# Keeping the low parts of the input weights in device memory between token blocks

## The chip, the cores and the metric

The kernel runs on one core of one Trainium2 chip. The metric is the device time of one execution in microseconds (us). The core has five engines with queues of their own: TensorE (PE in the profile, its weight loads PEld), VectorE (DVE), ScalarE (ACT), GpSimd (POOL) and SyncE (SP). SP issues every DMA of this kernel, in order, and 16 DMA engines carry them out.

## The reference

One inference step of a one-layer streaming encoder, for 2048 new frames with 16 meta tokens ahead of them, and for 32 frames of a running stream. All of it is float32.

```python
q, k, v, z_a, b_g, c_g, u, z_c = split_proj(rmsnorm(hp, norm_g[l]), w_in[l])   # 1024 -> 8 x 512
a = softmax(q1 k1/8 + bias) - lam * softmax(q2 k2/8 + bias)      # chunk-causal, 4 heads
o = rmsnorm(a @ v, subln_g) * 0.2 * silu(z_a)
y_c = silu(z_c) * b_g * conv3(c_g * u)                           # causal, width 3
hp = hp + concat(o, y_c) @ w_out                                 # then a final RMSNorm
```

The outputs are the two streams' results, the new keys and values, and the last two rows of the convolution's input.

## The kernel before, in words

**Split products.** TensorE multiplies in a reduced form of float32 (`F32R`). To keep the accuracy, each operand is split in two: a high part, the value cast to `F32R`, and a low part, the value minus the high part. A product is then three matmuls: high x high, high weight x low input, low weight x high input (lines 216 to 218).

**Blocks and columns.** The tokens are handled in four blocks (`p` = 0 to 3): the first holds the meta tokens, 512 frames and the 32 sample frames, the others 512 frames each. In every block all of `w_in` is used, in 32 columns of 128 output channels. One column is 1024 x 128 values, 512 KB, and 24 matmuls of 512 moving columns (in the first block 48 shorter ones). The order is written out in the main loop: for each head `h`, `unit_a` projects the columns q, k, v and z of that head (columns `h`, 4+`h`, 8+`h`, 12+`h`), `attend` does the attention of the block against all earlier keys, and `unit_c` projects four columns of the convolution branch. After the last block the output product (`out_first`, `out_rest`) follows.

**Weights.** `w_load(col, p)` brings in one column (line 190) into one of two `wraw` buffers and splits it in two halves of four 128 x 128 weight tiles each: ACT casts the high part `wh` (line 196), and then `wl = wr - wh` is made by POOL, or by DVE for the columns `CQ` and `CK` (0 and 4) in the first block and `CQ` and `CZ` (0 and 12) in the later ones (line 197). `wh` and `wl` have four buffers each, so two columns: the halves of column n go where those of column n-2 were, once PE has read them. The same is done anew in each of the four blocks.

**Attention.** For each tile of 128 frames and each chunk of keys, PE makes scores in one of three PSUM banks (lines 438, 439), DVE takes the row minimum (lines 385, 388), ACT the exponential out of the bank (line 389), which is what frees the bank. DVE makes the chunk's coefficients (lines 362 to 369), POOL and DVE combine the two softmaxes (lines 392, 393), PE transposes the result (line 454), ACT and DVE split it (lines 457, 458), and PE multiplies by the values (lines 461 to 463). Old keys and values are read back from device memory in each block (`ksd`, `vd`).

**What sets the order.** The kernel is written in Tile. The program order gives priorities, and a scheduler with a cost model of its own lays out a queue for each engine ahead of time (`schedule_with_timeline_sim=True`, line 798); it puts in the semaphores. Projections of the next columns and attention of the current head are so mixed on PE. On the chip each engine, SP too, goes through its queue strictly in that order.

In the trace, PE's first projection matmul of the second block is at about 258 us, of the third at 503, of the fourth at 788, and the output product starts to take over at 1073.

Of the kernel before, what the change touches and what calls it, by code (L numbers as in the profile page):

```python
# [11 lines left out]
F32 = mybir.dt.float32  # L12
F32R = mybir.dt.float32r
AF = mybir.ActivationFunctionType
ALU = mybir.AluOpType
AX = mybir.AxisListType

P = 128
D = 1024
KT = D // P  # L20
# [16 lines left out]
CQ, CK, CV, CZ, CB, CC, CU, CG = range(0, 32, 4)  # L37
# [10 lines left out]
def hybrid_step(ctx: ExitStack, tc: tile.TileContext, x, xT, ckT, cv, scT, rel_bias, norm_g, w_in,  # L48
# [10 lines left out]
    op = pool("op", 3)  # L59
# [3 lines left out]
    dram = pool("dram", 1, space=bass.MemoryType.DRAM)  # L63
# [5 lines left out]
    V, S, G, T = nc.vector, nc.scalar, nc.gpsimd, nc.tensor  # L69
    S.preload_act_table_set("natural_log_exp_and_others")  # L70
    f32 = lambda a: a.bitcast(F32) if a.dtype == F32R else a
    dma = lambda out, in_: nc.sync.dma_start(f32(out), f32(in_))
# [111 lines left out]


    pre = {}

    def w_load(col, p):
        wr = wp.tile([P, KT, P], F32, tag="wraw", name="wr")
        dma(wr, w_in[col])  # L190
        w2 = []
        for i in range(2):
            wh = wp.tile([P, KT // 2, P], F32R, tag="wh", name="wh", bufs=4)
            wl = wp.tile([P, KT // 2, P], F32R, tag="wl", name="wl", bufs=4)
            wi = wr[:, KT // 2 * i:KT // 2 * (i + 1)]
            S.copy(wh, wi)  # L196
            (V if (col in (CQ, CK) if p == 0 else col in (CQ, CZ)) else G).tensor_tensor(wl, wi, f32(wh), op=ALU.subtract)  # L197
            w2.append((wh, wl))
        return w2

    def proj(col, p, evac):
        w2 = pre.pop((col, p), None) or w_load(col, p)
        if p > 0:
            blks = [(0, QT)]
        elif col < CK or CZ <= col < CC or col >= CG:
            blks = [(NM, 288), (288, 560)]
        else:
            blks = [(0, 280), (280, 560)]
        for b0, b1 in blks:
            if p == 0 and col == CV:  # L210
                ps = ps_s.tile([P, 512], F32, tag="s", name="pj")[:, :b1 - b0]
            else:
                ps = ps_j.tile([P, 512], F32, tag="pj", name="pj")[:, :b1 - b0]
            for k in range(KT):
                wh, wl = w2[k // 4]
                for i, (a, b) in enumerate(((wh, xh), (wh, xl), (wl, xh))):
                    T.matmul(ps, lhsT=a[:, k % 4], rhs=b[k][:, b0:b1],  # L217
                             start=(k == 0 and i == 0), stop=(k == KT - 1 and i == 2))
            evac(ps, b0, b1)
# [508 lines left out]
    after = (((0,), (1,), (2, 3), ()), ((0,), (1,), (2,), (3,)))  # L728
    bias_rows()
    pre[CQ, 0] = w_load(CQ, 0)  # L730
    x_load(0)
    load_small()
# [73 lines left out]
```

## Time and profile before

| | |
|---|---|
| median of 3 runs | 1325.01 us (1324.07 to 1325.41) |
| the profiled execution | 1324.97 us |
| its span, first to last instruction | 1323.2 us |
| granted TensorE clock, mean over the span | 0.99 |
| DMA, mean over the span | 150 GB/s, 198.72 MB |
| device memory read, written | 145.62 MB, 43.26 MB |

The profile comes from one execution. Its busy times are unions of instructions on an engine. A matmul's end is modelled and matmuls overlap, so a busy PE is not a PE at its peak; idle time and the distance between starts say more. A row of a timeline has the start and the length in us, the engine, the line, the operation, the tiles written and read, and in brackets the idle time of the engine before it with what ended it.

### The profile page before, as it was taken

What the parts mean: (1) busy time and instruction counts of PE and PEld (TensorE: products, weight loads), DVE (VectorE), ACT (ScalarE), POOL (GpSimd) and SP (SyncE); (2) the same over time, 40 slices, a digit from 0 to 9 for tenths busy, and PEclk for the clock granted to TensorE, in tenths of its full rate; (3) what the DMA queues carried; (4) which work ended last, traced back from release to release, by engine and by line L of the source; (5) the groups of instructions that cost most, each with busy time, mean ns of one, the idle gap of its engine ahead of it and who ended that gap; (6) DMA issues with size and microseconds to landing.
All of it is one profiled execution on the core that took longest, in us unless ns stands there. A gap on an engine that the chain in (4) does not pass through costs nothing.

```text
span 1323.2 us, 21113 instructions
## 1 busy us (share of the span) xinstructions
PE 1279.3 (97%) x7058; PEld 1102.2 (83%) x7058; DVE 1011.5 (76%) x2086; ACT 738.0 (56%) x1854; POOL 731.3 (55%) x659
## 2 busy tenths in 40 slices
PE   8999999999999998999999999999999999999997
PEld 6999899988788886888888788888888887888775
DVE  8766567668797857788878868888798898856754
ACT  6645453664665547566565466565656665654322
POOL 4665655656566664466556656466666575642200
PEclk9999999999999999899999999999999999999999
DMA  9744434674335356534253463344334534557752
GB/s 285 219 141 108 138 99 113 205 243 145 121 105 174 106 159 192 169 127 151 96 168 102 135 194 100 124 131 124 105 104 153 161 110 128 159 183 231 231 176 90
DMA packets 108046, 198.72 MB, mean 150 GB/s; under 512 B 17409, under 2 KB 45601, under 8 KB 107937
## 3 DMA queue, kind: packets, MB, share of 16 engines
q1 hardware_dynamic: 107936, 197.37, 48.4%
q8 instruction: 55, 0.90, 0.3%
q14 instruction: 55, 0.44, 0.1%
HBM read 145.62 MB, written 43.26 MB: 143 GB/s over the span
## 4 chain that ended last, share of the span: by engine, by line
PE 30%; DVE 12%; ACT 3%; issue 2%; POOL 2%; DMA 1%; DVEq 0%; POOLq 0%; ACTq 0%
PE po L686 10%; PE pj L217 10%; DVE p L393 4%; PE pt L454 2%; PE s L438 2%; DVE nm L388 2%; PE s L439 2%; ACT p L389 1%; PE po L462 1%; PE po L463 1%; PE po L461 1%; DVE al L458 1%; POOL wl L197 1%; PE po L678 1%; DMA out<-y 0%
## 5 line engine op out<-in xcount | busy, mean ns | idle before, releaser
L217 PE MATMUL pj<-xh,wh 128*128 128x512 f32 (+2 forms) x1280 | 457.0, 358 | 3.8 <-DVE g L344 1.0
L217 PE MATMUL pj<-xl,wh 128*128 128x512 f32 (+2 forms) x1280 | 455.2, 356 | 1.7 <-DVE xl L145 1.7
L197 POOL TENSOR_TENSOR wl<-wr,wh 128x512 fp32r<-128x512 f32 x240 | 327.7, 1370 | 232.5 <-ACT wh L196 220.6
L217 PE MATMUL pj<-xh,wl 128*128 128x512 f32 (+2 forms) x1280 | 453.5, 355 | 0.0
L389 ACT ACTIVATE p<-s,nm 128x384 f32<-128x384 f32 (+5 forms) x352 | 208.6, 595 | 164.5 <-DVE nm L388 126.0
L217 PEld LDWEIGHTS pj<-xh,wh 128*128 128x128 f32 x1280 | 243.3, 190 | 35.4 <-ACT bvec L596 1.7
L217 PEld LDWEIGHTS pj<-xl,wh 128*128 128x128 f32 x1280 | 242.9, 190 | 30.9 <-DVE xl L145 3.2
L217 PEld LDWEIGHTS pj<-xh,wl 128*128 128x128 f32 x1280 | 242.8, 190 | 30.0 <-issue 1.1
L196 ACT CAST wh<-wr 128x512 fp32r<-128x512 f32 x256 | 157.1, 617 | 99.6 <-PE pj L217 61.4
L393 DVE SCALAR_TENSOR_TENSOR p<-p,cf,p 128x384 f32<-128x384 f32 (+5 forms) x176 | 176.6, 1025 | 21.9 <-POOL p L392 21.2
L392 POOL TENSOR_SCALAR p<-p,cf 128x384 f32<-128x384 f32 (+5 forms) x176 | 122.1, 709 | 60.6 <-DVE cf L369 42.1
L438 PE MATMUL s<-ks,q 128*128 128x384 f32 (+5 forms) x352 | 130.1, 371 | 12.0 <-ACT p L389 11.8
L388 DVE TENSOR_REDUCE nm<-s 128x1 f32<-128x384 f32 (+3 forms) x224 | 121.8, 557 | 2.8 <-PE s L439 2.6
L439 PE MATMUL s<-ks,q 128*128 128x384 f32 (+5 forms) x352 | 123.7, 352 | 0.0
L458 DVE TENSOR_TENSOR al<-pt,ah 128x512 fp32r<-128x512 f32 x144 | 97.0, 681 | 34.6 <-ACT ah L457 34.5
L666 POOL TENSOR_TENSOR cll<-ct,chh 128x512 fp32r<-128x512 f32 x40 | 55.9, 1404 | 108.6 <-ACT chh L664 108.6
L457 ACT CAST ah<-pt 128x512 fp32r<-128x512 f32 x144 | 80.8, 586 | 39.1 <-PE pt L454 36.7
L454 PE MATMUL pt<-ident,p 128*128 128x128 f32 x544 | 88.4, 274 | 1.6 <-DVE p L393 1.4
L438 PEld LDWEIGHTS s<-ks,q 128*128 128x128 f32 x352 | 66.7, 189 | 25.8 <-ACT p L389 18.7
L462 PE MATMUL po<-al,vh 128*128 128x256 f32 x288 | 83.5, 290 | 2.1 <-DVE al L458 2.0
L461 PE MATMUL po<-ah,vh 128*128 128x256 f32 x288 | 81.3, 282 | 0.0
L463 PE MATMUL po<-ah,vl 128*128 128x256 f32 x288 | 81.2, 282 | 0.0
(238 smaller groups left out, 2214.4 us busy)
## 6 DMA issues: line engine op xcount, KB each, us to landing
wr<-in_w_in SPq DMA_DIRECT2D x128, 512.0 KB, 3.7
ct<-cat SPq DMA_DIRECT2D x28, 512.0 KB, 4.6
q<-q SPq DMA_DIRECT2D x64, 128.0 KB, 2.8
out<-y SPq DMA_DIRECT2D x32, 256.0 KB, 3.7
ks<-ksd SPq DMA_DIRECT2D x8, 776.0 KB, 5.2
xr<-in_x SPq DMA_DIRECT2D x24, 256.0 KB, 5.3
out<-g SPq DMA_DIRECT2D x24, 256.0 KB, 2.9
xt<-in_xT SPq DMA_DIRECT2D x24, 256.0 KB, 4.7
```

What stands on the lines that cost most here:

```text
L196: S.copy(wh, wi)
L197: (V if (col in (CQ, CK) if p == 0 else col in (CQ, CZ)) else G).tensor_tensor(wl, wi, f32(wh), op=ALU.subtract)
L217: T.matmul(ps, lhsT=a[:, k % 4], rhs=b[k][:, b0:b1], start=(k == 0 and i == 0), stop=(k == KT - 1 and i == 2))
L388: V.tensor_reduce(nm[:, c, j:j + 1], s, op=ALU.min, axis=AX.X)
L389: S.activation(pr[j][c], s, AF.Exp, bias=nm[:, c, j:j + 1], scale=-1.0, accum_out=l[:, c, j:j + 1])
L392: G.tensor_scalar(a0, a0, cf[:, 0, j:j + 1], 1.0, op0=ALU.mult, op1=ALU.mult)
L393: V.scalar_tensor_tensor(a0, a1, cf[:, 1, j:j + 1], a0, op0=ALU.mult, op1=ALU.add)
L438: T.matmul(ps, lhsT=qd[c][0][:, qs], rhs=ks[c][:, col:col + w], start=True, stop=False)
L439: T.matmul(ps, lhsT=qd[c][1][:, qs], rhs=ks[c][:, col:col + w], start=False, stop=True)
L454: T.transpose(pt[:, i, P * qi:P * (qi + 1)], cols(aa[qi], NM + P * (2 * j + i), P), ident)
L458: V.tensor_tensor(al, pt, f32(ah), op=ALU.subtract)
L686: T.matmul(ps, lhsT=a[k][:, :rows], rhs=b[k], start=(k == 0 and i == 0), stop=(k == KT - 1 and i == 2))
```

## The change

32 tiles of 512 KB are set up in device memory, one for each column. In the second block (`p` = 1) each half of a low part is stored there after it is made. In the third and fourth block (`p` > 1) the low part is no longer computed: each half is loaded from there into the same `wl` buffer by a DMA. The first block is as before, and so are the load of the weights and the cast of the high part in all blocks. The `dma` helper issues on SP.

```diff
     pre = {}
+    wld = [dram.tile([2, P, KT // 2, P], F32, name=f"wld{c}", tag=f"wld{c}") for c in range(32)]
 
     def w_load(col, p):
         wr = wp.tile([P, KT, P], F32, tag="wraw", name="wr")
...
             wl = wp.tile([P, KT // 2, P], F32R, tag="wl", name="wl", bufs=4)
             wi = wr[:, KT // 2 * i:KT // 2 * (i + 1)]
             S.copy(wh, wi)
-            (V if (col in (CQ, CK) if p == 0 else col in (CQ, CZ)) else G).tensor_tensor(wl, wi, f32(wh), op=ALU.subtract)
+            if p > 1:
+                dma(wl, wld[col][i])
+            else:
+                (V if (col in (CQ, CK) if p == 0 else col in (CQ, CZ)) else G).tensor_tensor(wl, wi, f32(wh),
+                                                                                           op=ALU.subtract)
+            if p == 1:
+                dma(wld[col][i], wl)
             w2.append((wh, wl))
         return w2
```

## The prediction

> **What bounds the kernel now.** I read the page first, then the busy time by stage, then what TensorE (PE) waited for, and then the timeline around its longest wait.
>
> ```profile
> span 1323.2 us, 21113 instructions
> PE 1279.3 (97%) x7058; PEld 1102.2 (83%) x7058; DVE 1011.5 (76%) x2086; ACT 738.0 (56%) x1854; POOL 731.3 (55%) x659
> ```
>
> The execution took 1324.97 us: the span and 1.77 us around it. The median of the runs is 1325.01, so a sum made against this execution carries over. PE is the bound. POOL, which loses work here, is idle 45% of the time, so its time cannot be counted as gain. The windows view gives the busy time of each engine, the granted clock, and the share of the DMA engines with their rate, for the second block, the start of the third, the rest of the third, and the fourth:
>
> ```profile
> 258.00:503.00 245.00, 240.54 (x1202) 200.92 (x1203) 191.03 (x401) 143.57 (x358) 152.87 (x130) 0.99 0.50 154
> 503.00:545.00 42.00, 35.49 (x150) 28.54 (x150) 31.58 (x76) 25.86 (x73) 19.16 (x17) 0.88 0.66 216
> 545.00:788.00 243.00, 238.40 (x1262) 203.49 (x1261) 197.92 (x380) 142.90 (x349) 145.47 (x127) 1.00 0.43 136
> 788.00:1073.00 285.00, 282.56 (x1497) 242.15 (x1496) 245.73 (x464) 178.26 (x441) 177.61 (x156) 1.00 0.41 123
> ```
>
> One row stands out: from 503 to 545 us PE is idle for 6.5 of 42 us and its clock is 0.88. Elsewhere in the two blocks that read back, it idles 4.6 and 2.4 us. That is all there is to win: about 13.5 us of idle time and what the clock loses. What these waits end on (total, times, longest), first for the third block, then for the fourth:
>
> ```profile
> PE s L438 <- ACT p L389: 6.6, 5, 3.3
> PE ptv L308 <- DVE g L297: 1.7, 1, 1.7
> PE po L462 <- DVE al L458: 1.3, 1, 1.3
> PE pj L217 <- DVE g L344: 1.0, 1, 1.0
> PE pt L454 <- DVE p L393: 0.4, 1, 0.4
> ```
>
> ```profile
> PE ptv L308 <- DVE g L297: 1.3, 1, 1.3
> PE s L438 <- ACT p L389: 0.5, 1, 0.5
> PE pj L217 <- DVE xl L145: 0.5, 1, 0.5
> ```
>
> No row names wl: the low parts were never late. Every row ends on VectorE (DVE) or on ScalarE (ACT) behind it: the softmax chain (row minimum on DVE, exp on ACT, then a score bank is free) and the copies out of PSUM. So the change can pay only through DVE's lateness.
>
> **What is removed.** The subtraction at L197, by count and by block (second, third, fourth; DVE's part, then POOL's):
>
> ```profile
> L197 POOL TENSOR_TENSOR wl<-wr,wh 128x512 fp32r<-128x512 f32 x240 | 327.7, 1370 | 232.5 <-ACT wh L196 220.6 <-PE pj L217 3.6 <-PE s L439 2.1
> ```
>
> ```profile
> 258.00:503.00 245.00, 4.11 (x4) 82.97 (x61) 0.99 0.50 154
> 503.00:788.00 285.00, 3.83 (x4) 82.24 (x60) 0.98 0.46 148
> 788.00:1073.00 285.00, 2.37 (x2) 81.89 (x60) 1.00 0.41 123
> ```
>
> Two blocks have 2 x 64 = 128 subtractions, 120 on POOL and 8 on DVE (columns 0 and 12). POOL loses 120 x 1.37 = 164 us, half of its work there; DVE loses 8 x 0.95, about 7 us. POOL's part also holds DVE up. The timeline shows it:
>
> ```profile
> 517.27 1.30 POOL L197 TENSOR_TENSOR wl<-wr,wh 128x512 fp32r<-128x512 f32 x1 [1.68 <-ACT wh L196]
> 517.48 1.11 DVE L368 TENSOR_TENSOR r<-r,lam 128x2 f32<-128x2 f32 x1
> 520.58 1.78 DVE L197 TENSOR_TENSOR wl<-wr,wh 128x512 fp32r<-128x512 f32 x1
> 525.01 0.68 DVE L197 TENSOR_TENSOR wl<-wr,wh 128x512 fp32r<-128x512 f32 x1
> 526.95 0.57 DVE L388 TENSOR_REDUCE nm<-s 128x1 f32<-128x400 f32 x1
> 527.55 0.59 ACT L389 ACTIVATE p<-s,nm 128x400 f32<-128x400 f32 x1 [1.71 <-DVE nm L388]
> 528.28 0.59 PE L438 MATMUL s<-ks,q 128*128 128x272 f32 x1 [3.28 <-ACT p L389]
> 529.21 0.16 DVE L368 TENSOR_TENSOR r<-r,lam 128x2 f32<-128x2 f32 x1
> 530.91 0.60 PE L438 MATMUL s<-ks,q 128*128 128x272 f32 x1 [1.80 <-ACT p L389]
> 534.10 0.63 PE L217 MATMUL pj<-xh,wl 128*128 128x512 f32 x1
> 534.53 0.63 PE L217 MATMUL pj<-xh,wh 128*128 128x512 f32 x1
> ```
>
> The same two-element product takes 1.11 us beside a POOL subtraction and 0.16 without one. And the longest wait of the run has two of DVE's own subtractions (1.78 and 0.68) ahead of the row minimum at 526.95, whose exp at 527.55 frees the bank for which PE waits 3.28 us, till 528.28. A second wait of 1.80 follows, and then the clock:
>
> ```profile
> 526.60:536.80 10.20, 6.71 (x19) 5.34 (x20) 9.23 (x29) 4.97 (x15) 4.99 (x7) 0.50 1.01 335
> 150.00:154.50 4.50, 3.56 (x17) 3.26 (x18) 1.90 (x4) 1.84 (x5) 3.16 (x5) 0.63 0.61 175
> ```
>
> For 10.2 us PE has half its clock; matmuls start 0.43 us apart (534.10, 534.53). From 530.91 to 536.8 it works without a gap, 5.9 us that would be 2.9 at full clock: 3.0 us lost. The stretch costs 3.28 + 1.80 + 3.0 = 8.1 us.
>
> *Gain there.* Without the two subtractions DVE's queue is 1.78 + 0.68 = 2.46 us shorter ahead of the minimum; without POOL's at 517.27 the product at 517.48 gives back 1.11 - 0.16, nearly 1.0. That is 3.4 us off the 5.08 us of waits. What is late next is POOL's other work (lines 252 and 278), which also blocks DVE, so the waits do not vanish. Half of the clock's 3.0 should go with them, since a shorter wait may still cost clock: at 150 us a stretch with 0.9 us of idle PE inside it (a wait begun before it) shows 0.63. Total 3.4 + 1.5, say 5 us; bounds 0 (the order is redrawn and another chain is late here) and 8.1.
>
> [...]
>
> *Gain elsewhere.* The other waits are 11.0 - 5.1 = 5.9 us in the third block and 2.3 in the fourth, 8.2 together. They hang on DVE, and POOL's work, whose readers block it, is halved. But the planner lays out a new order for every engine, and new waits come with it; I take a quarter, 2 us (bounds: 8 gained, 4 lost, the size of what the rest of the third block idles now).
>
> **What is added.** In the second block 64 stores of 256 KB, in the third and fourth 128 loads of 256 KB, all on SP. Nearest rows: loads of that size (the whole run's bz, the third block's xr), a store of that size, and one store's issue on SP:
>
> ```profile
> bz<-bz SPq DMA_DIRECT2D x16, 256.0 KB, 3.8
> xr<-in_x SPq DMA_DIRECT2D x6, 256.0 KB, 5.7
> vd<-vl SPq DMA_DIRECT2D x12, 256.0 KB, 4.2
> 528.25 0.43 SPq L72 DMA_DIRECT2D ksd<-ks  x1
> ```
>
> *Stores.* 64 x 0.43 = 28 us of SP's time in 245. Each waits for the POOL subtraction of its half; the next weight load, which SP issues about then, waits for the same subtractions already, so little queued behind is held longer: the q copies, old keys and outputs. The low part's buffer now stays taken until the store has landed, 0.43 + 4.2 after the subtraction, while PE reads it later still (below). Cost 0.5 us (bounds -1 and +4).
>
> *Loads.* A load can start when PE has done with the buffer's last user two columns before, and must land before the third matmul of its half. PE's end of one such use and its first use of the refilled buffer, the closest pair that I found in the third block:
>
> ```profile
> 738.23 0.39 PE L217 MATMUL pj<-xh,wl 128*128 128x512 f32 x1
> 748.23 0.39 PE L217 MATMUL pj<-xh,wl 128*128 128x512 f32 x1
> ```
>
> From 738.62 to 748.23 are 9.6 us. Issue and landing take 0.43 + 3.8 to 0.43 + 5.7, so 3.5 to 5.4 us are spare: cost 0, hidden by the column between. If that cover is gone, each late load is a wait of PE. What eats it is SP, which issues in order (third and fourth block):
>
> ```profile
> SPq L72 <- POOL wl L197: 236.9, 49, 11.6
> SPq L72 <- POOL o L422: 33.0, 7, 10.9
> ```
>
> The first row's waits change their cause: the weight load waits for the cast alone, and the low-part loads for PE. The second shows what a load may be queued behind: 4.7 us on average, 10.9 at most.
>
> **Sum.** 1324.97 - 5 - 2 + 0.5 = 1318.5 us.
>
> **Rivals.**
>
> *The waits only move.* PE's wait for a score bank or a PSUM copy is part of a queue order that is drawn up anew; a DVE that is earlier in one place is idle there and late at another (it is busy 246 of 285 us in the fourth block, where PE still idles just 2.4). For it: wl appears in no wait of PE. Against: the longest wait has the subtractions in its chain. Gain and loss cancel: 1324.5.
>
> *Low parts late, slower.* Place: SP in the third and fourth block, a wl load queued behind a store that waits for POOL or DVE. With 3.5 us spare an average wait of 4.7 makes it 1.2 late, the longest 7.4. From about 9 us in all (the 6.5 us gained and 2.65 more) it decides. Two loads 5 us late, each with a half-clock window (half of 3.4, 1.7 us, the length of such a window taken as a third of the 10.2) cost 13.4: 1318.5 + 13.4 = 1332. Against: most columns have more than 9.6 us, since attention matmuls lie between.
>
> *Transfers bound.* The third block would go from 148 by 16.8 MB / 285 us = 59 to 207 GB/s, well under the 335 reached; but the window from 526.6 is full already (1.01). Two columns' 1 MB there are 3.1 us more at that rate; if PE waits for them and the gain there is lost too, 1324.97 + 3.1 + 0.5, about 1329. Against: prefetches for the fourth block fill that window, and PE's next weights are already in.
>
> [...]
>
> **Chances.** Forecast 0.50; waits only move 0.22; low parts late 0.17; transfers bound 0.06; and 0.05 that nearly all of the 13.5 us and the clock's 3.0 go, about 1309. A measurement of this kernel can tell 0.2%, 2.65 us, from no change: faster 0.55, same 0.22, slower 0.23. The forecast's own range is 1313 to 1322, from its bounds; the range that holds 8 in 10 reaches through the second and fourth case and into the third: 1311 to 1330.
>
> **What would show it.** L197 leaves POOL after about 503 us (POOL near 570 us in all, L197 on POOL x120, on DVE x8); DVE's time falls by more than its own 7 us, with L368 and L393 shorter; PE's 3.28 us wait shrinks and the half clock at the third block's start is shorter or gone; no wait of PE on a DMA of wl; 33.6 MB more read and 16.8 MB more written. Wrong if PE's idle time in the last two blocks stays near 13.5 us though DVE is freed, or if PE rows end on "DMA wl", or if the second block grows by more than 4 us.

## The result and the profile after

The median went from 1325.21 us (1324.07 to 1325.97, 4 runs) to 1307.88 us (1307.37 to 1309.48, 4 runs): 17.3 us less, ratio 0.987 with a 95% interval of 0.9855 to 0.9886. The direction was forecast, the size was not: the time lies below the forecast's range. Of all the runs in this document one was slow, 1555 us at 0.75 of the clock (the kernel in which only the fourth block reads), and the ratios leave it out. The profiled execution took 1309.48 us, 1.8 of it around the span. The page of the kernel after, its span and busy times, and the memory traffic:

```profile
span 1307.7 us, 21292 instructions
PE 1275.0 (98%) x7058; PEld 1103.9 (84%) x7058; DVE 935.7 (72%) x2078; ACT 741.6 (57%) x1854; POOL 562.1 (43%) x539
wl<-wld SPq DMA_DIRECT2D x128, 256.0 KB, 2.8
wld<-wl SPq DMA_DIRECT2D x64, 256.0 KB, 2.5
HBM read 179.17 MB, written 60.04 MB: 183 GB/s over the span
```

POOL lost 169 us of work, and DVE became 76 us shorter, though only eight operations of its own are gone. The span fell by 15.5 us: PE's idle time (span less busy) from 43.9 to 32.7, and its busy time by 4.3, with the same 7058 matmuls: they stand closer together, part of it because less of the time has half clock. By block, cut where the second, third and fourth block's columns and then the output product begin, first the kernel before (its first cut is another than in the prediction), then after:

```profile
258.00:505.50 247.50, 242.02 (x1208) 201.97 (x1209) 193.53 (x406) 144.14 (x358) 154.59 (x131) 0.99 0.51 155
505.50:787.60 282.10, 272.01 (x1403) 230.67 (x1402) 226.60 (x451) 167.79 (x419) 162.50 (x143) 0.98 0.46 147
787.60:1073.30 285.70, 283.26 (x1499) 242.76 (x1498) 246.43 (x464) 178.66 (x442) 178.31 (x156) 1.00 0.41 123
1073.30:1323.20 249.90, 235.12 (x1137) 192.32 (x1135) 169.91 (x350) 113.94 (x301) 84.65 (x71) 0.98 0.53 168
```

```profile
258.00:505.70 247.70, 242.43 (x1210) 201.97 (x1210) 190.54 (x405) 144.42 (x358) 149.83 (x129) 0.99 0.69 225
505.70:776.40 270.70, 267.93 (x1404) 230.49 (x1403) 194.05 (x449) 169.58 (x419) 83.80 (x84) 0.99 0.66 215
776.40:1062.70 286.30, 285.05 (x1517) 245.37 (x1516) 215.40 (x470) 182.60 (x449) 94.68 (x97) 1.00 0.58 180
1062.70:1307.70 245.00, 232.31 (x1119) 190.66 (x1118) 159.94 (x339) 112.00 (x293) 82.08 (x69) 0.98 0.53 169
```

The second block, which now stores, is as long as before. The third is 11.4 us shorter. The fourth is as long but does 18 matmuls more, which the output stage then does not have (1119 for 1137); that stage is 4.9 shorter. What PE waits for from 503 to 776 us is one row, and from 776 to 1062 two:

```profile
PE s L445 <- ACT p L396: 2.8, 1, 2.8
```

```profile
PE po L468 <- ACT o L425: 0.8, 1, 0.8
PE ptv L315 <- DVE g L304: 0.3, 1, 0.3
```

No row ends on the loads. The stretch that stood out, and the half clock that is left in it:

```profile
503.00:545.00 42.00, 39.14 (x184) 32.54 (x183) 28.83 (x81) 30.18 (x82) 9.20 (x10) 0.96 0.83 278
528.20:531.60 3.40, 3.40 (x15) 3.21 (x15) 3.32 (x9) 2.59 (x8) 0.00 (x0) 0.50 1.05 399
```

PE idles 2.9 us there instead of 6.5, and has half clock for 3.4 us instead of 10.2. Why DVE got faster shows in operations that the change does not touch. From 503 to 1063 us, the combination of the two softmaxes and the two-element product, before and after:

```profile
L393 DVE SCALAR_TENSOR_TENSOR p<-p,cf,p 128x384 f32<-128x384 f32 (+3 forms) x103 | 104.9, 1040 | 10.7 <-POOL p L392 10.7
L368 DVE TENSOR_TENSOR r<-r,lam 128x2 f32<-128x2 f32 x31 | 13.5, 436 | 0.8
```

```profile
L400 DVE SCALAR_TENSOR_TENSOR p<-p,cf,p 128x384 f32<-128x384 f32 (+3 forms) x107 | 85.3, 825 | 6.4 <-POOL p L399 6.4
L375 DVE TENSOR_TENSOR r<-r,lam 128x2 f32<-128x2 f32 x31 | 7.3, 235 | 0.6
```

The mean fell from 1040 to 825 ns and from 436 to 235 ns: DVE had been held up inside its instructions. The timeline from 503 to 1075 us shows beside what. Before, the two-element product took 0.16 us where no POOL operation ran (19 of 31) and 0.92 us in the mean, up to 1.27, where one of POOL's subtractions ran at the same time (6). The row minimum of 400 columns, which reads a score bank and no second tile, took 0.56 us either way. POOL's lines 252 and 278, which the change leaves in, held DVE up too: over the whole span before, L393 with 512 columns took 1.77 us beside the one and 1.78 beside the other (once each), and 0.73 where no POOL operation ran (11 times).

### The profile page after: what moved, and what is told of

Its sections match the earlier page's. It is cut to its first block, busy times and chain, and to the rows that moved or that the text cites. A ratio compares the mean times of both kernels' runs of the same rounds, so it can differ in the third digit from the quotient of the medians.

```text
span 1307.7 us, 21292 instructions
## 1 busy us (share of the span) xinstructions
PE 1275.0 (98%) x7058; PEld 1103.9 (84%) x7058; DVE 935.7 (72%) x2078; ACT 741.6 (57%) x1854; POOL 562.1 (43%) x539
## 4 chain that ended last, share of the span: by engine, by line
PE 61%; DVE 4%; DMA 4%; ACT 3%; POOL 1%; issue 1%; DVEq 0%; SPq 0%; ACTq 0%; POOLq 0%
PE pj L224 32%; PE po L693 9%; PE pt L461 4%; PE s L445 4%; PE s L446 4%; PE po L469 2%; PE po L470 2%; PE po L468 2%; DMA ct<-cat 2%; DMA out<-y 1%; DVE p L400 1%; ACT p L396 1%; PE po L685 1%; DVE nm L395 0%; DMA wr<-in_w_out 0%
## 5 line engine op out<-in xcount | busy, mean ns | idle before, releaser
L201 POOL TENSOR_TENSOR wl<-wr,wh 128x512 fp32r<-128x512 f32 x120 | 161.6, 1353 | 83.3 <-ACT wh L197 70.6
L400 DVE SCALAR_TENSOR_TENSOR p<-p,cf,p 128x384 f32<-128x384 f32 (+5 forms) x176 | 149.6, 876 | 18.9 <-POOL p L399 18.4
L392 DVE CUSTOM_DVE_ANT_0 s<-s,bz 128x512 f32<-128x512 f32 (+5 forms) x128 | 74.2, 589 | 22.5 <-PE s L446 19.6
```

What stands on the lines that cost most here:

```text
L400: V.scalar_tensor_tensor(a0, a1, cf[:, 1, j:j + 1], a0, op0=ALU.mult, op1=ALU.add)
```

## The experiments

Theories: **A1**, POOL's subtraction, while it reads its two tiles, holds up DVE, and the softmax chain is late by that. **A2**, POOL's queue was too full. **B**, the gain is only the new order that the planner drew up. **C**, wl came late. **D**, DVE's own two subtractions ahead of the longest wait, the main term of my sum, are what counts. Ratios are to the kernel before, run on the same chip. The diffs are shortened to what matters, and are against the kernel after where nothing else is said. The planner draws up each kernel's order anew, so a single run seldom parts B from the rest; the tables at the end do.

### Load, and subtract all the same

```diff
             if p > 1:
                 dma(wl, wld[col][i])
+                (V if col in (CQ, CZ) else G).tensor_tensor(wi, wi, f32(wh), op=ALU.subtract)
```

> Stores and loads as in the change, but in the third and fourth block the 128 subtractions are still done by the same engines, into the raw weights, which nobody reads any more. Theory A (the gain comes from the subtractions that POOL and DVE no longer do): 1322 to 1328 us, DVE's time back above 1000 us. Rival B (the gain is only the new order that the planner drew up once wl came by DMA): 1306 to 1312 us. Rival C (it is the wait of wl for the cast, that is the chain raw weights, cast, subtraction, that was too long): 1306 to 1312 us as well.

1339.35 us, ratio 1.011 (1.0095 to 1.0125). With the subtractions back the gain is gone, though wl still comes by DMA: C falls. B's forecast failed too, but this order is again another. Theory A's forecast of the time was missed as well, for the kernel takes 14 us more than the one before, with the same work on DVE:

```profile
PE 1284.6 (96%) x7058; PEld 1105.6 (83%) x7058; DVE 1008.6 (75%) x2086; ACT 739.2 (55%) x1854; POOL 732.7 (55%) x659
```

### Fill POOL's queue, without reading

```diff
             if p > 1:
                 dma(wl, wld[col][i])
+                if col not in (CQ, CZ):
+                    for _ in range(3):
+                        G.memset(wi, 0.0)
```

> As the change, but in the third and fourth block POOL writes zeros three times over the raw weights of each half that it no longer subtracts, 120 x 3 fills: about as long on POOL as the subtractions (a fill of 256 columns took 307 ns, so some 0.5 us each), in the same queue places, but without reading. Theory A1 (POOL's reading holds up DVE's operations on two tiles): 1307 to 1312 us, DVE near 936 us. Theory A2 (POOL's queue was too full, its L392 came late behind subtractions): 1318 to 1326 us with DVE near 936 us all the same.

1306.1 us, ratio 0.986 (0.9844 to 0.9877): the whole gain, with POOL busier than before the change. The page's busy times, and the fills by line from 503 us on:

```profile
PE 1272.1 (98%) x7058; PEld 1102.5 (85%) x7058; DVE 950.9 (73%) x2078; ACT 741.1 (57%) x1854; POOL 748.7 (58%) x899
```

```profile
L203 POOL MEMSET wr<- 128x512 f32 x358 | 189.1, 533 | 148.6 <-ACT wh L198 134.7 <-issue 2.3 <-POOL q L262 0.3
```

189 us of POOL's time in these blocks cost nothing: A2 falls. What POOL is busy with matters, not that it is busy. DVE is 15 us busier than in the change all the same. Part of it is beside the fills: an operation of 512 columns with one tile read (line 180 of the kernel before) took 0.56 us in the mean beside them (9 times) and 0.42 beside no POOL operation (6). Where the rest comes from is not shown.

### Read one tile on POOL

Against the kernel with the fills:

```diff
-                        G.memset(wi, 0.0)      # three times
+                        G.tensor_scalar(wi, wi, 1.0, 1.0, op0=ALU.mult, op1=ALU.mult)      # twice
```

> As the kernel with POOL's fills, but instead of three fills two operations that read the raw half and write it back, on POOL, about 0.85 us each: POOL's time like that of the subtractions, one tile read. Theory A1 (it is POOL's reading that holds DVE): DVE above 980 us, 1318 to 1335 us. Rival (the fills were harmless since nothing waits for them): DVE near 945 us, 1303 to 1310 us.

1315.35 us, ratio 0.9931 (0.9913 to 0.9949), between the two forecasts, with DVE below what A1 forecast:

```profile
PE 1274.9 (97%) x7058; PEld 1102.4 (84%) x7058; DVE 964.3 (74%) x2078; ACT 739.9 (56%) x1854; POOL 731.2 (56%) x779
```

```profile
L202 POOL TENSOR_SCALAR wr<-wr 128x512 f32<-128x512 f32 x238 | 170.4, 718 | 157.6 <-ACT wh L197 145.0 <-issue 1.5 <-POOL q L261 1.3
```

About the same POOL time, 170 us, holds DVE up more than fills do and less than subtractions with two tiles read (DVE 964.3 us, for 950.9 with the fills and 1000.5 with POOL's subtractions but not DVE's eight, below). The two-element product shows it too: beside fills, which read nothing, it took 0.16 us (12 times), as alone; beside these one-tile copies 0.25 us in the mean (11 times); beside subtractions, before, 0.92. The 8 us of the median are less sure than these durations, since another order can move it as far (below).

### DVE's eight alone, and POOL's 120 alone

```diff
-            if p > 1:
+            if p > 1 and col in (CQ, CZ):          # the other kernel: col not in (CQ, CZ)
                 dma(wl, wld[col][i])
...
-            if p == 1:
+            if p == 1 and col in (CQ, CZ):         # the other kernel: col not in (CQ, CZ)
                 dma(wld[col][i], wl)
```

> Only the two columns whose low parts DVE makes (0 and 12) are stored and read back; POOL subtracts as before. Theory A1 (POOL's reading holds up DVE): 1319 to 1324 us, since only DVE's own 7 us go. Theory D (DVE's own two subtractions ahead of the longest wait are what counts): 1313 to 1317 us, with the half clock near 527 us gone.

1321.41 us, ratio 0.9969 (0.9958 to 0.998).

> Only the 30 columns whose low parts POOL makes are stored and read back; DVE makes its two as before. Theory A1: 1308 to 1314 us. Theory D: 1317 to 1323 us, with the 10 us of half clock near 527 us still there.

1306.3 us, ratio 0.9866 (0.9839 to 0.9892). The score banks' wait from 503 to 560 us (with POOL's 120 gone there is a second wait), and the half clock near 527 us, with DVE's eight gone and then with POOL's 120 gone:

```profile
PE s L444 <- ACT p L395: 5.5, 2, 3.3
525.60:535.80 10.20, 7.06 (x20) 5.59 (x21) 9.16 (x25) 4.95 (x15) 4.74 (x6) 0.50 1.01 316
```

```profile
PE s L444 <- ACT p L395: 2.1, 1, 2.1
PE pt L460 <- DVE p L399: 1.0, 1, 1.0
527.90:531.30 3.40, 3.31 (x14) 3.12 (x15) 3.30 (x11) 2.65 (x9) 0.00 (x0) 0.50 1.01 385
```

The longest wait stays when DVE's two subtractions ahead of it leave, and it shrinks when they stay and POOL's go. D falls: an instruction that stands in the chain is not for that the cause of the lateness.

### What stores and loads cost

```diff
-            if p > 1:
+            if False:              # stores only: every block subtracts
                 dma(wl, wld[col][i])
```

> The second block stores the low parts, nobody reads them; every block subtracts as before. Stores hidden (the change's second block took the same 247 us as before): 1322 to 1328 us. Rival (the stores hold buffers and SP, and the relief pays for it): 1329 to 1335 us.

1322.49 us, ratio 0.9983 (0.9972 to 0.9995): no cost. In the traces PE's 7058 matmuls and POOL's 659 operations come in the very order of the kernel before, so this comparison is free of B. Yet its stretch from 503 to 545 us, with every subtraction in it, is milder, with 6.8 us of half clock in place of 10.2 and no wait longer than 2.0 us:

```profile
503.00:545.00 42.00, 37.30 (x171) 30.92 (x172) 32.88 (x83) 27.85 (x76) 20.85 (x19) 0.92 0.68 226
PE s L441 <- ACT p L392: 4.0, 2, 2.0
```

So a part of the 3.28 us wait went with no work taken from DVE or POOL.

```diff
                 dma(wl, wld[col][i])
+                dma(wi, wld[col][i])       # each low part a second time
```

> As the change, and each low part is loaded a second time, into the raw weights, where nobody reads it: 128 more loads on SP and 33.6 MB more. Loads hidden: 1305 to 1311 us. Rival (loads and SP's order cost, as the kernels suggest that load and subtract): 1313 to 1322 us.

1307.66 us, ratio 0.9873 (0.9855 to 0.9891). 256 loads are hidden as well as 128, with DVE at 935.6 us.

```diff
-            if p > 1:
-                dma(wl, wld[col][i])
+            if p > 1:              # subtract into wl as before, then load over the raw half
+                dma(wi, wld[col][i])
```

> All subtractions into wl as before, the stores as in the change, and in the third and fourth block the 128 loads go into the raw weights after their subtraction, where nobody reads them: the traffic and SP's issues without any relief. Theory A1 with hidden loads: 1322 to 1328 us. Rival for the 1339 us of the kernel that loads and subtracts (the loads themselves cost, and the relief gives more than the 17 us seen): 1333 to 1342 us.

1331.27 us, ratio 1.0053 (1.0037 to 1.0069). The same traffic without relief is 6.7 us slower than the kernel before, between the two forecasts. Here the load also keeps a raw buffer, so this run alone does not part a cost of loads from one of the order.

### Another order, the same work

```diff
-            (V if (col in (CQ, CK) if p == 0 else col in (CQ, CZ)) else G).tensor_tensor(...)
+            (V if (col in (CQ, CK) if p == 0 else col in ((CQ, CZ) if p == 1 else (CQ + 1, CZ + 1))) else G).tensor_tensor(...)
```

This is the kernel before, without stores or loads; DVE takes other columns.

> The kernel before, with no stores and no loads: in the third and fourth block DVE subtracts the second unit's columns 1 and 13 instead of the first unit's 0 and 12. Every engine has the same work; the planner's order is another. It asks whether 1339 and 1331 us of the kernels that subtract and load are a matter of order. If the time without relief hangs on the order: outside 1322 to 1328 us, most likely 1328 to 1336 us. If it does not, and the loads cost there: 1322 to 1328 us. Theory D (DVE's own subtractions in the longest wait): 1316 to 1321 us, since they leave that place.

1333.28 us, ratio 1.0068 (1.0051 to 1.0084), with DVE at 1003.5 us. What PE waited for from 500 to 1085 us begins with these rows:

```profile
PE s L438 <- ACT p L389: 9.1, 8, 4.3
PE pt L454 <- DVE p L393: 2.7, 4, 1.3
PE ptv L308 <- DVE g L297: 2.1, 3, 0.8
```

So another order of the same work can cost 9 us without relief, in the same waits. That is the part of B that is true: of the five kernels with every subtraction the kernel before is the second fastest, behind the stores alone, which have its order.

### The fourth block alone, and the second too

```diff
-            if p > 1:
+            if p > 2:
```

> Stores as in the change, only the fourth block reads; the third subtracts as before. The change's gain lay in the third block (11 us of the PE's lost time, 1.4 in the fourth, 2.8 behind it): 1319 to 1324 us if the gain is where the waits were. Rival (each block that reads gains half): 1313 to 1317 us.

1317.28 us, ratio 0.9942 (0.9926 to 0.9957): near the rival, half of the gain for half of the relief (DVE 968.0 us), though the fourth block of the kernel before showed almost no wait. But not all of it came from the block that reads. The start of the third block, which subtracts as before, lost less than before, with 3.4 us of half clock:

```profile
503.00:545.00 42.00, 37.25 (x174) 30.62 (x173) 33.23 (x83) 28.18 (x77) 21.40 (x19) 0.96 0.68 230
PE s L444 <- ACT p L395: 3.7, 3, 2.1
```

In the table by block below, 3.3 us of this run's gain lie in the third block and 4.5 from the fourth on. The rival's number came out and its reason only in part.

```diff
-            if p > 1:                    # loads from the second block on,
+            if p > 0:
...
-            if p == 1:                   # stores in the first
+            if p == 0:
```

> The first block stores and all three later blocks read. Theory A1 (POOL's reading holds up DVE): the second block, whose PE loses 14.5 us beyond its matmuls' distance, loses 6 to 9 instead, as the fourth does in the change: 1299 to 1304 us. Rival (order only, or the second block's waits do not hang on DVE): 1306 to 1312 us. Rival (the first block's DMA, at 0.55 of its engines already, and SP cannot take the stores): 1310 to 1320 us.

1306.35 us, ratio 0.9867 (0.9853 to 0.9882), a number that the first rival gave. Its reason is not borne out: counted by projection matmuls (1536 in the first block, 768 in each later one), the second block took 240.4 us for 246.8 in the change, as A1 had it, and the first 263.1 for 258.3. DVE fell to 905.5 us, but the first block now ends late. From 20 to 40 us the DMA engines were full already in the change (first row); with the stores on top PE gets through 142 matmuls for 149 (second row, this kernel):

```profile
20.00:40.00 20.00, 19.80 (x149) 19.17 (x149) 14.28 (x44) 12.65 (x32) 12.53 (x12) 1.00 1.00 327
```

```profile
20.00:40.00 20.00, 19.47 (x142) 18.68 (x142) 13.99 (x44) 10.29 (x27) 9.56 (x10) 1.00 1.02 347
```

```diff
+            w = 1 if col % 4 == 0 else 0     # the first unit's columns are stored one block later
-            if p > 1:
+            if p > w:
...
-            if p == 1:
+            if p == w:
```

> The first block stores the 24 columns of the units after the first, the second block the 8 columns of the first unit; later blocks read. It keeps the stores out of the first 60 us, whose DMA engines were full (1.02 of their time from 20 to 40 us) when the first block stored all. Theory (the second block's relief, 6.4 us, was partly paid for by 4 us in the first block's start): 1300 to 1304 us. Rival (the first block's loss comes from anywhere in it): 1305 to 1309 us.

1299.1 us, ratio 0.981 (0.9794 to 0.9826): the fastest of all, 26 us under the kernel before, with the first block back at 258.6 us. Its page, and its second block, in which PE idles 0.4 us:

```profile
PE 1269.0 (98%) x7058; PEld 1100.8 (85%) x7058; DVE 911.4 (70%) x2078; ACT 742.3 (57%) x1854; POOL 494.9 (38%) x491
258.00:500.00 242.00, 241.60 (x1223) 203.29 (x1223) 170.46 (x411) 146.44 (x363) 84.82 (x81) 1.00 0.73 235
```

### All of them by DVE's busy time

| kernel | DVE busy, us | median, us |
|---|---|---|
| before; stores only | 1011.5; 1008.5 | 1325.2; 1322.5 |
| load and subtract; dead loads; other columns | 1008.6; 1008.3; 1003.5 | 1339.4; 1331.3; 1333.3 |
| DVE's eight gone | 1000.5 | 1321.4 |
| fourth block alone; POOL reads one tile | 968.0; 964.3 | 1317.3; 1315.4 |
| fills; POOL's 120 gone | 950.9; 942.7 | 1306.1; 1306.3 |
| the change; loads twice | 935.7; 935.6 | 1307.9; 1307.7 |
| mostly from the first block; all from it | 911.4; 905.5 | 1299.1; 1306.4 |

Above 1000 us of DVE the time spreads over 18 us; in the four kernels from 935 to 951 us it spreads over 2, though PE's orders there are three (without POOL's 120 it is nearly the change's). By block the profiled executions, one each, read as follows. A block begins with its first projection matmul, counted as 1536 of the first block and 768 of each later one; the last column is the fourth block and the output stage together, since orders move matmuls between them.

| kernel | third block, us | fourth and output, us |
|---|---|---|
| before; stores only (the same order) | 282.3; 279.7 | 536.0; 535.9 |
| load and subtract; dead loads; other columns | 278.9; 279.4; 277.9 | 551.5; 545.7; 547.6 |
| DVE's eight gone; fourth block alone | 278.9; 279.0 | 539.7; 531.5 |
| POOL reads one tile; fills | 270.9; 271.2 | 534.8; 525.4 |
| POOL's 120 gone; the change; loads twice | 271.1; 270.8; 269.6 | 527.5; 531.7; 529.2 |

Whatever the order, the third block takes 278 to 282 us where POOL subtracts in it, and 270 to 271 where it does not, whether DVE makes its eight (POOL's 120 gone) or POOL is busy with fills. With the durations above this is what A1 rests on. It is some 8 us of the change's 11.5 there; the other 3 are what the kernel before took above its like. One-tile copies cost nothing in this block. From the fourth block on the time hangs on the order as well. The three kernels that are slower than the kernel before lose there, and one of them has no loads, which speaks for the order and against a cost of loads, but does not prove it. Three things stay open: why the kernel that loads and subtracts is the worst of the orders, how much of the dead loads' 6.7 us is order, and how much of the 8 us of the one-tile copies is.

## Why the prediction was wrong

*PE bound, POOL's time no gain in itself.* Right: the fills put it all back for nothing.

*Stores and loads hidden.* Right, and more so than bounded: the loads landed in 2.8 us at the median, not 3.8 to 5.7, and twice as many were hidden too. The rivals of late low parts and of bound transfers fall.

*Gain at the third block's start, 5 us.* Somewhat too much: the two waits of 5.08 us became one of 2.8, and half clock on a busy PE cost 1.7 us (half of 3.4) instead of 3.0; 3.6 in all. The reason was wrong: 2.46 of my 3.4 us were DVE's own subtractions, and without them alone the stretch kept its 3.3 us wait and its 10.2 us of half clock. What shortened it is not shown: with POOL's 120 gone it is shorter, but so it is in the two kernels that subtract everything there in other timings (stores alone, fourth block alone).

*Gain elsewhere, 2 us.* This is the step that failed. The span shows 15.5 - 3.6 = 11.9 us, some 8 of it in the rest of the third block and 4 in the fourth block and the output stage. I bounded the term by PE's listed waits in the two blocks (8.2), called that all there was to win, and then took a quarter, because a new order brings new waits. That is so as long as DVE is held up (1333 us with other columns), but with DVE free the new orders have hardly any: of the 8.2 us some 7 went, 5.9 to none in the third block and 2.3 to 1.1 in the fourth. And the bound itself left out what no wait row shows: the output stage, whose idle time fell by 2.1 us (14.8 to 12.7), and about 3.0 us of PE's busy time (4.3 less the clock's 1.3) in which matmuls stood further apart without a gap between busy times. What held those apart is not shown.

*The range and the case of 1309.* The range of 1313 to 1322 was narrower than the bounds it was said to come from: at their best they give 1324.97 - 8.1 - 8 - 1 = 1307.9. That this is the measured time is luck, as is the nearness of the case of 1309, which had 0.05: of its 13.5 us of idle time 9.4 went and of the clock's 3.0 only 1.3, and what is missing came from where it did not look.

*The waits only move.* Fell as the outcome of this change. It is what happens to a change of order without relief.

*The clock.* The half-clock stretches read here are 3.4, 6.8 or 10.2 us long. The 3.4 us that the rival of late low parts counted with, a third of the 10.2, also stands in the kernel before by itself:

```profile
338.90:342.30 3.40, 3.00 (x12) 2.81 (x13) 3.40 (x9) 1.38 (x4) 1.47 (x1) 0.50 0.17 54
```

Shorter waits still came with half clock: after the change a wait of 2.8 us, and with POOL's part gone waits of 2.1 and 1.0 with matmuls between, each time with 3.4 us of it. To have kept half of that gain was right: 1.5 us were taken, 1.3 came.

## What to carry to other kernels

When VectorE feeds the engine that bounds, look at the mean time of its small two-tile operations: if a two-element product takes 436 ns in the mean and 160 alone, look whether the long ones run beside GpSimd operations that read tiles, as here (0.92 us beside subtractions, 0.25 beside one-tile copies, 0.16 beside fills). If so, part of VectorE's busy time hangs on GpSimd's, and taking elementwise work off GpSimd can be worth more than its own wait rows show: with POOL's 120 subtractions gone DVE was busy for 942.7 us instead of 1011.5, and the ratio was 0.9866. Judge a removal by what the removed work does to its neighbours, not by its place in the chain. And where a planner lays out the order, one kernel's waits are one draw: before costing a wait, ask how the time would move with another order, and compare block by block over several of them.

## What was not expected of the hardware

Some 160 to 190 us of GpSimd time in the last two blocks cost 0 us as fills, 8 us as one-tile copies (part of it perhaps order) and 13 us as subtractions of two tiles, each against the change; VectorE's own eight are gone in all of them. And 84 MB of added traffic (33.6 x 2 read, 16.8 written), on a kernel that moved 199 MB, cost nothing against the change's 50; only stores at the start of the first block did cost, some 5 us.
